# Gate rows of a two-direction mLSTM: one chain over all tokens, or two parts placed by hand

## The chip, the cores and the metric

The kernel runs on one core of one Trainium2 chip. The metric is the time of one execution on the device in microseconds (us), the median over several runs.

## The reference, cut to what matters

One layer of a diffusion backbone acts on 1024 latent tokens (a grid) and 256 context tokens of width 1024. Both are normalised, modulated and projected by one matrix; three branches (pooling, spatial gating, mLSTM) follow, then a merge and a feed-forward part. The change is in the mLSTM branch: four heads, two scan directions, chunked. Its gates, two numbers per token, head and direction, go through the following, in which `b` is a running sum inside a chunk and `m` a running maximum over all chunks:

```python
gp = gate_pre.astype(f32) + b_gates.astype(f32)
i_f, i_b, f_f, f_b = jnp.split(gp, 4, axis=-1)
logf_f = jax.nn.log_sigmoid(f_f)
...
b = jnp.cumsum(fc, axis=1)
dmat = b[:, :, None, :] - b[:, None, :, :] + ic[:, None, :, :]
dmat = jnp.where(causal[None, :, :, None], dmat, -jnp.inf)
inter = b + m[:, None, :]
m_t = jnp.maximum(inter, jnp.max(dmat, axis=2))
w_intra = jnp.exp(dmat - m_t[:, :, None, :])
w_inter = jnp.exp(inter - m_t)
...
w_state = jnp.exp(bL[:, None, :] - b + ic - m_new[:, None, :])
decay = jnp.exp(bL + m - m_new)
```

The head's output is multiplied by `sigmoid(o_pre)`, the output gate. The latent scan starts from a cached state, the context scan from zero.

## The kernel before, in words

Tokens lie in three groups (`GROUPS`): 0 and 1 hold 512 latent (sample) tokens each, 2 holds the 256 context tokens. The normalised input is kept transposed as `uT`, eight blocks of 128 features for each group, each split into a high and a low part, because every product is three matmuls in a narrow float format (`dense`, L117 to 125): high by high, high by low, low by high. A weight block comes by one transfer on SP's queue (`fetch_w`), is rounded to its high part by ScalarE (`A.copy`, L93) and its low part is taken by VectorE (L94). Two raw buffers and three pairs of high and low parts exist (`NRAW`, `NHL`). `dense` writes one of three PSUM banks (`ps_mm`), which ScalarE evicts; transposes and small products use five others (`ps_sd`).

What sets the order: a scheduler reads the program, plays it against a model of the engines and writes each engine's instructions in the order in which they became ready there; among those that are ready the earlier in the program goes first. `Pinned` (L35 to 45) takes that freedom away: an instruction issued through it is queued behind whatever stood before it in the program on its engine. From L258 to L411 the names `V`, `A`, `G`, `PE` are pinned, so that stretch runs in the order in which it is written, and whatever is issued without the wrapper may be put between. All pinned instructions carry the wrapper's line, L43, in the profile.

The pinned stretch computes the modulation, fills `uT` and has k and v of head 0 (`p_k`, `p_v`) multiplied as `uT` comes in. The loop at L376 goes over `steps`: the eight blocks of group 1, then the eight of group 2 (the context steps). A step issues the transposes of the step four ahead (`tr`), the scaling of the step two ahead (`mc`) and six matmuls of k and v. At context step 0 the gates of groups 0 and 1 are multiplied (`gates_of`), copied out by ScalarE (`pgs`) and partly moved to other partitions by a transfer (`pgl`, L357); at context step 3 `gates_add` joins the parts into two rows of `z`. Behind the loop come the evictions of k and v and the gates of group 2.

At L412 the pinning ends. The gate rows' chain (L413 to 470) then runs over all 1280 tokens at once, on 36 partitions (rows 0 to 3 for the forward direction, 32 to 35 for the backward one): Abs, Sigmoid, Exp, Ln on ScalarE, arithmetic and scans on VectorE; the log-sigmoid's correction term is multiplied by the Sigmoid (L421, L426). `zi`, `z5` and `z4` are the three results. Each is transposed in 10 pieces on TensorE (`pc`, L478) and copied into `gcol` by VectorE; a small product (`pd`, L491) spreads two rows of 10 chunks each to all partitions. Then `rhl` splits one more row for later use.

The heads follow (L532 to 662): `head_proj` multiplies what is missing of k, v, q (for head 0 the second and third group of q), and `head` transposes k and v (`tk`, `tv`), sums the states (`kv`), multiplies scores and values (`st`, `rb`, `pv`), and at group 0 of each head issues the output gate's projection (L647, `p_o`), whose eviction `ev_o` writes the Sigmoid into `so`. All of this is the scheduler's to place: where TensorE would wait in its model, it takes matmuls of later program lines.

Of the kernel before, what the change touches and what calls it, by code (L numbers as in the profile page):

```python
# [48 lines left out]
def hybrid_step(  # L49
# [28 lines left out]
    def ps_sd(name):  # L78
        return pp.tile([P, 512], F32, tag="sd", name=name, bufs=5)
# [258 lines left out]
    nc.gpsimd.dma_start(sel, sel8)  # L338

    R36 = 36  # L340
    zr = [z[0:R36, i * T : (i + 1) * T] for i in range(7)]

    gparts = {}

    def gates_of(g):


        t0, n = GROUPS[g]
        pg = ps_sd(f"pg{g}")
# [26 lines left out]
    for at, (g, k) in enumerate(steps):  # L376
# [38 lines left out]
    def chunks(ap):
        return ap.rearrange("p (c t) -> p c t", t=P)

    zi, zf, z2, z3, z4, z5, z6 = zr
    V.tensor_scalar(zf, zf, bgt[:, 1:2], None, ALU.add)
    A.activation(z2, zf, AF.Abs)  # L420
    A.activation(z6, z2, AF.Sigmoid)  # L421
    A.activation(z2, z2, AF.Exp, scale=-1.0)
    V.tensor_scalar(z3, z2, 1.0, None, ALU.add)
    A.activation(z4, z3, AF.Ln)
    V.scalar_tensor_tensor(z5, z3, -1.0, z2, ALU.add, ALU.subtract)
    V.tensor_tensor(z5, z5, z6, ALU.mult)  # L426
    V.tensor_tensor(z4, z4, z5, ALU.subtract)
    V.scalar_tensor_tensor(zf, zf, 0.0, z4, ALU.min, ALU.subtract)
    G.memset(z4, 1.0)
    G.memset(chunks(z4)[0:32, :, 0:1], 0.0)  # L430
    G.memset(chunks(z4)[32:36, :, 127:128], 0.0)
    rev = slice(None, None, -1)
    V.tensor_tensor_scan(z2[0:32], z4[0:32], zf[0:32], 0.0, ALU.mult, ALU.add)
    V.tensor_tensor_scan(z2[32:36, rev], z4[32:36, rev], zf[32:36, rev], 0.0, ALU.mult, ALU.add)
    for lo_, hi_, smp in ((0, NSAMP, True), (NSAMP, T, False)):
        ini = m0t if smp else None
        V.tensor_tensor_scan(
            z3[0:32, lo_:hi_], zf[0:32, lo_:hi_], zi[0:32, lo_:hi_],
            ini[0:32] if smp else 0.0, ALU.add, ALU.max)
        V.tensor_tensor_scan(  # L440
            z3[32:36, lo_:hi_][:, rev], zf[32:36, lo_:hi_][:, rev], zi[32:36, lo_:hi_][:, rev],
            ini[32:36] if smp else 0.0, ALU.add, ALU.max)
    bL = cp.tile([R36, NT], F32, name="bL")
    mnew = cp.tile([R36, NT], F32, name="mnew")
    mprev = cp.tile([R36, NT], F32, name="mprev")
    V.memset(mprev, 0.0)
    b3, m3 = chunks(z2), chunks(z3)
    V.tensor_copy(bL[0:32], b3[0:32, :, 127])
    V.tensor_copy(bL[32:36], b3[32:36, :, 0])
    V.tensor_copy(mnew[0:32], m3[0:32, :, 127])  # L450
    V.tensor_copy(mnew[32:36], m3[32:36, :, 0])
    V.tensor_copy(mprev[0:32, 0:1], m0t[0:32])
    V.tensor_copy(mprev[0:32, 1:8], mnew[0:32, 0:7])
    V.tensor_copy(mprev[0:32, 9:10], mnew[0:32, 8:9])
    V.tensor_copy(mprev[32:36, 7:8], m0t[32:36])
    V.tensor_copy(mprev[32:36, 0:7], mnew[32:36, 1:8])
    V.tensor_copy(mprev[32:36, 8:9], mnew[32:36, 9:10])
    G.dma_start(m_out[0], mnew[0:4, 9:10])
    G.dma_start(m_out[1], mnew[32:36, 8:9])
    bm = cp.tile([R36, NT], F32, name="bm")  # L460
    V.tensor_tensor(bm, bL, mnew, ALU.subtract)
    dec = cp.tile([R36, NT], F32, name="dec")
    V.tensor_tensor(dec, bm, mprev, ALU.add)
    A.activation(dec, dec, AF.Exp)

    V.tensor_tensor(zi, zi, z2, ALU.subtract)
    V.tensor_tensor(z2, z2, z3, ALU.subtract)
    A.activation(z5, z3, AF.Exp, scale=-1.0)
    V.tensor_tensor(chunks(z4), chunks(zi), bm.unsqueeze(2).to_broadcast([R36, NT, P]), ALU.add)
    A.activation(z4, z4, AF.Exp)  # L470


    gcol = cp.tile([P, 3, NT, 8], F32, name="gcol")
    for qi, src in enumerate((zi, z5, z4)):
        pc = ps_sd(f"pc{qi}")
        pcv = pc[:, 0 : NT * R36].rearrange("p (c j) -> p c j", j=R36)
        for c in range(NT):
            PE.transpose(pcv[:, c, :], src[:, c * P : (c + 1) * P], ident[0:R36, 0:R36])  # L478
        for d in range(2):
            V.tensor_copy(gcol[:, qi, :, 4 * d : 4 * d + 4], pcv[:, :, 32 * d : 32 * d + 4])  # L480
    GC, EM, EWS = (gcol[:, i] for i in range(3))

    dsel = tmp("dsel")[0:R36, 0:160].rearrange("p (q j c) -> p q j c", q=2, j=8)
    for qi, src in enumerate((dec, mprev)):
        V.tensor_tensor(
            dsel[:, qi], src.unsqueeze(1).to_broadcast([R36, 8, NT]),
            sel[0:36, :].unsqueeze(2).to_broadcast([R36, 8, NT]), ALU.mult)
    ones36 = tmp("ones36")[0:R36, 0:P]
    V.memset(ones36, 1.0)
    pd = ps_sd("pd")  # L490
    PE.matmul(pd[:, 0:160], ones36, dsel.rearrange("p q j c -> p (q j c)"), start=True, stop=True)  # L491
# [44 lines left out]
    so = z[:, 7730:9010]  # L536
# [18 lines left out]
    def head(h, kT, vT, qT):  # L555
# [980 lines left out]
```

## Time and profile before

| what | us |
|---|---|
| median of three runs | 1947.19 (1946.92 to 1949.57) |
| the profiled execution | 1947.31 |
| its span, first to last instruction | 1945.5 |
| TensorE busy in the span | 1903.0 |
| VectorE busy | 1294.0 |
| ScalarE busy | 861.7 |
| mean granted clock of TensorE | 0.994 of full |

Times inside the trace count from the span's first instruction. In the rows PE is TensorE, DVE VectorE, ACT ScalarE, POOL GpSimd, SP the queue that issues most transfers. A row of a timeline gives the start, the length, the engine, the line of the kernel, the operation with what it writes and reads, and in brackets how long the engine was idle before it and what ended that. Consecutive lengths on TensorE overlap, so the distance of two starts is the price of a matmul. The clock of a window is a share of full speed: TensorE has two levels, 2.4 GHz (1.00) and 1.2 GHz (0.50).

### The profile page before, as it was taken

The numbers are of one execution on the slowest core, as the hardware profiler recorded it, in microseconds if no ns is written. First come the engines' busy times: TensorE is split into PE (matmuls) and PEld (weight loads), VectorE is DVE, ScalarE is ACT, GpSimd is POOL, SyncE is SP. The second block draws the span as 40 slices with busy tenths as digits, with TensorE's granted clock in tenths as the row PEclk, the third lists the DMA queues.
The fourth block names the chain that finished last, engine by engine and source line by source line (L and its number), as shares of the span: only waits on it lengthen the run. The fifth ranks groups of instructions, "written<-read, shape, count | busy, mean of one in ns | idle before, by whom it ended". The sixth has DMA issues, their size and how long they took to land.

```text
span 1945.5 us, 28129 instructions
## 1 busy us (share of the span) xinstructions
PE 1903.0 (98%) x10136; PEld 1627.5 (84%) x10136; DVE 1294.0 (67%) x2207; ACT 861.7 (44%) x1768; POOL 378.2 (19%) x380
## 2 busy tenths in 40 slices
PE   6999999999999999999999999999999999999998
PEld 3778888998788888888888887888888888888886
DVE  6574443347759889875675599888776655744665
ACT  7444464653243333343123374555454545443443
POOL 1200001107302424220000015444431110000003
PEclk9999999999999999999999999999999999999999
DMA  9211111012635445469522435776773586654444
GB/s 361 85 59 33 43 39 40 27 56 70 203 119 165 149 158 164 153 211 321 163 97 98 152 120 212 253 264 246 259 269 136 193 333 203 210 170 151 165 133 159
DMA packets 149318, 313.32 MB, mean 161 GB/s; under 512 B 17550, under 2 KB 40818, under 8 KB 147130
## 3 DMA queue, kind: packets, MB, share of 16 engines
q1 hardware_dynamic: 107354, 220.73, 33.9%
q0 software_dynamic: 15520, 57.75, 7.8%
q10 hardware_dynamic: 26304, 33.04, 4.7%
q8 instruction: 79, 1.29, 0.3%
q14 instruction: 61, 0.50, 0.1%
HBM read 217.59 MB, written 93.36 MB: 160 GB/s over the span
## 4 chain that ended last, share of the span: by engine, by line
PE 87%; DVE 4%; DMA 3%; POOL 2%; ACT 1%; issue 1%; SPq 0%; POOLq 0%; ACTq 0%; DVEq 0%
PE w L1403 6%; PE w L1404 6%; PE w L1405 6%; PE pb L1050 3%; PE pb L1051 3%; PE pb L1052 3%; PE fT L892 3%; PE fT L890 3%; PE fT L891 3%; PE fB L891 2%; PE fB L890 2%; PE fB L892 2%; PE fT_g L892 2%; PE fT_g L890 2%; PE fT_g L891 2%; PE po L1168 2%
## 5 line engine op out<-in xcount | busy, mean ns | idle before, releaser
L1242 POOL TENSOR_TENSOR z<-z 128x512 f32<-128x512 f32 x64 | 100.1, 1564 | 123.3 <-DMA z<-in_w_ff 120.6
L947 DVE TENSOR_TENSOR z<-z 128x512 f32<-128x512 f32 x112 | 88.7, 792 | 2.5
L527 POOL PARTITION_ALL_REDUCE acc<-acc x16 | 54.6, 3446 | 184.0 <-DVE acc L521 113.6
L521 DVE SCALAR_TENSOR_TENSOR acc<-z,scond,acc 128x512 f32<-128x512 f32 x112 | 86.1, 816 | 0.0
L1357 POOL TENSOR_TENSOR rs_y<-rs_y,neghalf 128x1 f32<-128x1 f32 x10 | 9.6, 966 | 333.0 <-DVE rs_y L1356 333.0
L1208 ACT ACTIVATE z<-z 128x512 f32<-128x512 f32 x64 | 40.5, 632 | 69.8 <-DVE z L956 36.7
L972 ACT ACTIVATE z<-z 128x512 f32<-128x512 f32 x48 | 30.3, 632 | 59.1 <-DVE z L956 23.1
L130 POOL TENSOR_TENSOR rs_h<-rs_h,neghalf 128x4 f32<-128x4 f32 (+1 forms) x12 | 10.9, 910 | 200.5 <-DVE rs_h L129 200.3
L653 DVE SCALAR_TENSOR_TENSOR yc<-th,ccol,z 128x512 f32<-128x512 f32 (+1 forms) x12 | 7.9, 661 | 58.2 <-PE th L651 58.2
L1056 DVE TENSOR_TENSOR sg<-pb,sg 128x512 f32<-128x512 f32 (+1 forms) x48 | 28.7, 600 | 26.7 <-PE pb L1052 26.5
L881 ACT CAST hi_wb<-raw_wb 128x512 fp32r<-128x512 f32 x24 | 14.8, 620 | 64.4 <-PE pb L1051 37.6
L1209 ACT ACTIVATE z<-z 128x512 f32<-128x512 f32 x64 | 40.3, 629 | 1.1
L1171 DVE TENSOR_TENSOR po<-po,gt 128x512 f32<-128x512 f32 (+1 forms) x24 | 14.6, 607 | 35.1 <-PE po L1170 35.0
L1233 POOL DMA_DIRECT2D scr_s<-x x48 | 26.3, 549 | 53.1 <-DVE x L1227 47.6
L738 POOL TENSOR_TENSOR z<-z 128x1024 f32<-128x1024 f32 (+13 forms) x20 | 33.6, 1702 | 6.9 <-ACT z L722 4.6
L528 POOL TENSOR_TENSOR acc<-acc,bt 1x512 f32<-1x512 f32 x16 | 23.5, 1480 | 58.4 <-issue 58.4
L1174 ACT ACTIVATE po<-z 128x512 f32<-128x512 f32 (+1 forms) x24 | 12.7, 529 | 48.5 <-DVE z L1173 34.2
L587 DVE SCALAR_TENSOR_TENSOR z<-z,dmb,kv 128x129 f32<-128x129 f32 x56 | 16.6, 345 | 21.8 <-PE kv L576 21.3
L1057 DVE TENSOR_TENSOR z<-z,sg 128x512 f32<-128x512 f32 (+1 forms) x48 | 28.7, 601 | 1.2
L640 DVE TENSOR_TENSOR den<-den,gcol 128x2 f32<-128x2 f32 x40 | 6.2, 159 | 31.0 <-ACT den L639 29.9
L43 PE MATMUL pm<-wah,shl 128*4 128x512 f32 x32 | 13.8, 461 | 13.2 <-ACT wah L43 13.2
L130 POOL TENSOR_TENSOR rs_f<-rs_f,neghalf 128x4 f32<-128x4 f32 (+1 forms) x3 | 3.3, 1092 | 116.9 <-DVE rs_f L129 116.9
(5136 smaller groups left out, 7288.9 us busy)
## 6 DMA issues: line engine op xcount, KB each, us to landing
z<-in_w_ff SPq DMA_DIRECT2D x64, 512.0 KB, 5.5
z<-in_w_ada SPq DMA_DIRECT2D x64, 256.0 KB, 3.1
scr_t<-z POOLq DMA_DIRECT2D x16, 1024.0 KB, 4.9
z<-in_w_in SPq DMA_DIRECT2D x24, 512.0 KB, 4.3
scr_g<-z ACTq DMA_DIRECT2D x48, 256.0 KB, 2.0
sg<-scr_g SPq DMA_DIRECT2D x48, 256.0 KB, 4.5
scr_h<-z ACTq DMA_DIRECT2D x48, 256.0 KB, 3.6
scr_s<-x POOLq DMA_DIRECT2D x48, 256.0 KB, 4.3
```

Of the source, the lines that this page charges most:

```text
L521: V.scalar_tensor_tensor(acc[j], raw, scond[:, k, j : j + 1], acc[j], ALU.mult, ALU.add)
L890: PE.matmul(ps, whi[:, s], ahi, start=first and k == ks[0], stop=False)
L891: PE.matmul(ps, whi[:, s], alo, start=False, stop=False)
L892: PE.matmul(ps, wlo[:, s], ahi, start=False, stop=end and k == ks[-1])
L947: V.tensor_tensor(out, x, y, op)
L1050: PE.matmul(pb[:, :n], whi[:, s], yh, start=kc == 0, stop=False)
L1051: PE.matmul(pb[:, :n], whi[:, s], yl, start=False, stop=False)
L1052: PE.matmul(pb[:, :n], wlo[:, s], yh, start=False, stop=kc == 3)
L1242: G.tensor_tensor(out, x, y, ALU.subtract)
L1403: PE.matmul(banks[j], h_[:, s], rh, start=fp == 0, stop=False)
L1404: PE.matmul(banks[j], l_[:, s], rh, start=False, stop=False)
L1405: PE.matmul(banks[j], h_[:, s], rl, start=False, stop=fp == NFP - 1)
```

## The change

The gate rows' chain becomes ten small functions that take a part: `SMP` (groups 0 and 1, 1024 tokens) or `CTXT` (group 2, 256 tokens). The pinned stretch is lengthened over the whole chain, over the rest of q0, over head 0's output gate (`o0`, taken out of `head(0)`) and over head 1's k (`k1`, taken out of `head_proj(1)` by way of `begun`), so the order between these is the one written. The sample part's first steps stand at context step 6; its transposes stand between `o0` and `k1`, those of the context part behind `k1`. The Sigmoid of the log-sigmoid's correction and its multiplication are left out, and seven rows of `z` become six. The row of ones in the running sum is written by POOL earlier, and the loads and splits of the weights of `o0` and `k1` are traced inside the pinned stretch, but not pinned themselves.

```diff
-    zr = [z[0:R36, i * T : (i + 1) * T] for i in range(7)]
+    zr = [z[0:R36, i * T : (i + 1) * T] for i in range(6)]
...
+    def part(groups):
+        lo_, hi_ = GROUPS[groups[0]][0], sum(GROUPS[groups[-1]])
+        return slice(lo_ // P, hi_ // P), [t[:, lo_:hi_] for t in zr]
+
+    SMP, CTXT = (0, 1), (2,)
...
+    def g_join(groups):
+        for g in groups:
+            gates_add(g)
+        V.tensor_scalar(yf, yf, bgt[:, 1:2], None, ALU.add)
+        engines[2].memset(y4, 1.0)
+        engines[2].memset(chunks(y4)[0:32, :, 0:1], 0.0)
+        engines[2].memset(chunks(y4)[32:36, :, 127:128], 0.0)
+    def g_exp(groups):
+        A.activation(y2, yf, AF.Abs)
+        A.activation(y2, y2, AF.Exp, scale=-1.0)
+    def g_one(groups):
+        V.tensor_scalar(y3, y2, 1.0, None, ALU.add)
+        V.scalar_tensor_tensor(y5, y3, -1.0, y2, ALU.add, ALU.subtract)
+    def g_log(groups):
+        A.activation(y3, y3, AF.Ln)
+    def g_logf(groups):
+        V.tensor_tensor(y3, y3, y5, ALU.subtract)
+        V.scalar_tensor_tensor(yf, yf, 0.0, y3, ALU.min, ALU.subtract)
+    def g_max(groups):
+        for r, d in scan_dirs():
+            V.tensor_tensor_scan(
+                y3[r][:, d], yf[r][:, d], yi[r][:, d], m0t[r] if groups is SMP else 0.0, ALU.add, ALU.max)
+    def g_sum(groups):
+        cc, (yi, yf, y2, y3, y4, y5) = part(groups)
+        c0, c1 = cc.start, cc.stop
+        for r, d in scan_dirs():
+            V.tensor_tensor_scan(y2[r][:, d], y4[r][:, d], yf[r][:, d], 0.0, ALU.mult, ALU.add)
+        b3, m3 = chunks(y2), chunks(y3)
+        V.tensor_copy(bL[0:32, cc], b3[0:32, :, 127])
+        V.tensor_copy(bL[32:36, cc], b3[32:36, :, 0])
+        V.tensor_copy(mnew[0:32, cc], m3[0:32, :, 127])
+        V.tensor_copy(mnew[32:36, cc], m3[32:36, :, 0])
+        if groups is SMP:
+            V.tensor_copy(mprev[0:32, 0:1], m0t[0:32])
+            V.tensor_copy(mprev[32:36, 7:8], m0t[32:36])
...
+        V.tensor_tensor(bm[:, cc], bL[:, cc], mnew[:, cc], ALU.subtract)
+        V.tensor_tensor(dec[:, cc], bm[:, cc], mprev[:, cc], ALU.add)
+    def g_em(groups):
+        A.activation(y5, y3, AF.Exp, scale=-1.0)
+    def g_diff(groups):
+        cc, (yi, yf, y2, y3, y4, y5) = part(groups)
+        V.tensor_tensor(yi, yi, y2, ALU.subtract)
+        V.tensor_tensor(
+            chunks(y4), chunks(yi), bm[:, cc].unsqueeze(2).to_broadcast([R36, cc.stop - cc.start, P]), ALU.add)
+        V.tensor_tensor(y2, y2, y3, ALU.subtract)
+    def g_last(groups):
+        cc, (yi, yf, y2, y3, y4, y5) = part(groups)
+        A.activation(y4, y4, AF.Exp)
+        A.activation(dec[:, cc], dec[:, cc], AF.Exp)
+    def gate_columns(groups):
+        cc, (yi, yf, y2, y3, y4, y5) = part(groups)
+        c0, nch = cc.start, cc.stop - cc.start
+        for qi, src in enumerate((yi, y5, y4)):
+            pc = ps_sd(f"pc{qi}_{c0}")
+            pcv = pc[:, 0 : nch * R36].rearrange("p (c j) -> p c j", j=R36)
+            for c in range(nch):
+                PE.transpose(pcv[:, c, :], src[:, c * P : (c + 1) * P], ident[0:R36, 0:R36])
+            for d in range(2):
+                V.tensor_copy(gcol[:, qi, cc, 4 * d : 4 * d + 4], pcv[:, :, 32 * d : 32 * d + 4])
+        dsel = tmp(f"dsel{c0}")[0:R36, 0 : 16 * nch].rearrange("p (q j c) -> p q j c", q=2, j=8)
+        for qi, src in enumerate((dec, mprev)):
+            V.tensor_tensor(
+                dsel[:, qi], src[:, cc].unsqueeze(1).to_broadcast([R36, 8, nch]),
+                sel[0:36, :].unsqueeze(2).to_broadcast([R36, 8, nch]), ALU.mult)
+        ones36 = tmp(f"ones36_{c0}")[0:R36, 0:P]
+        V.memset(ones36, 1.0)
+        pd = ps_sd(f"pd{c0}")
+        PE.matmul(pd[:, 0 : 16 * nch], ones36, dsel.rearrange("p q j c -> p (q j c)"), start=True, stop=True)
+        V.tensor_copy(
+            dmb[:, :, :, cc], pd[:, 0 : 16 * nch].rearrange("p (q j c) -> p q j c", q=2, j=8))
 
...
-        if (g, k) == (2, 3):
-            gates_add(0)
-            gates_add(1)
+        if (g, k) == (2, 6):
+            g_join(SMP)
+            g_exp(SMP)
+            g_one(SMP)
+            g_log(SMP)
+            g_logf(SMP)
...
+    def ev_o(g, ps):
+        t0, n = GROUPS[g]
+        A.activation(so[:, t0 : t0 + n], ps[:, :n], AF.Sigmoid)
+    def q0_part(g):
+        ps = ps_mm(f"p_q0{g}")
+        dense(ps, w_q0, uT, g)
+        begun["q0"][1].append(evict_kqv("q", 0, g, ps, kq0))
+    def o0_part(g):
+        ps = ps_mm(f"p_o0{g}")
+        dense(ps, w_o0, uT, g)
+        ev_o(g, ps)
+    pinned, (V, A, G, PE) = (V, A, G, PE), engines
+    kq1 = slot("kq1", F32)
+    w_o0 = load_w(w_in[I_O], "o0")
+    w_k1 = load_w(w_in[I_K + 1], "k1")
+    begun["k1"] = w_k1, []
+    V, A, G, PE = pinned
+    g_join(CTXT)
+    g_exp(CTXT)
+    g_max(SMP)
+    g_one(CTXT)
+    g_sum(SMP)
+    q0_part(1)
+    q0_part(2)
+    g_log(CTXT)
+    g_em(SMP)
+    g_diff(SMP)
+    o0_part(0)
+    g_last(SMP)
+    o0_part(1)
+    o0_part(2)
+    gate_columns(SMP)
+    g_logf(CTXT)
+    g_max(CTXT)
+    g_sum(CTXT)
+    g_em(CTXT)
+    g_diff(CTXT)
+    g_last(CTXT)
+    for g in range(3):
+        ps = ps_mm(f"p_k1{g}")
+        dense(ps, w_k1, uT, g)
+        begun["k1"][1].append(evict_kqv("k", 1, g, ps, kq1))
+    gate_columns(CTXT)
     V, A, G, PE = engines
-    gates_add(2)
...
-    A.activation(z6, z2, AF.Sigmoid)
...
-    V.tensor_tensor(z5, z5, z6, ALU.mult)
...
-            if g == 0:
+            if g == 0 and h > 0:
                 proj(I_O + h, f"o{h}", ev_o)
```

## Rows read from the trace of the kernel before

**Rows 1.** Page, part 1: busy time, share of the span and instructions of each engine.
```profile
PE 1903.0 (98%) x10136; PEld 1627.5 (84%) x10136; DVE 1294.0 (67%) x2207; ACT 861.7 (44%) x1768; POOL 378.2 (19%) x380
```

**Rows 2.** Waits of TensorE, 60 to 160 us: us in total, times, longest.
```profile
PE pc L478 <- DVE z L466: 3.6, 1, 3.6
...
PE p_v L43 <- ACT kT L43: 1.1, 1, 1.1
...
PE p_k L123 <- ACT z L597: 0.3, 1, 0.3
```

**Rows 3.** Windows: busy us by engine, granted clock, DMA share, GB/s.
```profile
80.00:90.00 10.00, 8.94 (x53) 7.71 (x52) 2.62 (x7) 4.64 (x10) 0.00 (x0) 1.00 0.15 43
...
130.00:135.00 5.00, 1.38 (x16) 1.20 (x15) 4.80 (x12) 0.00 (x0) 1.07 (x2) 0.98 0.01 0
...
135.00:140.00 5.00, 5.00 (x26) 4.64 (x26) 4.97 (x15) 2.39 (x4) 0.00 (x0) 0.50 0.08 16
...
140.00:145.00 5.00, 5.00 (x26) 3.86 (x26) 2.14 (x3) 0.31 (x2) 0.00 (x0) 0.84 0.32 87
```

**Rows 4.** Timeline of TensorE, 85 to 147 us: start, length, line, operation, idle before.
```profile
88.65 0.48 PE L43 MATMUL p_k<-u2c,hi_k 128*128 128x256 f32 x2
...
89.58 0.47 PE L123 MATMUL p_q<-u0h,hi_q 128*128 128x512 f32 x1
...
98.75 0.40 PE L43 MATMUL pg<-u0c,wgs 128*128 128x256 f32 x2
...
100.67 0.28 PE L123 MATMUL p_q<-u0c,hi_q 128*128 128x256 f32 x1
...
103.56 0.40 PE L123 MATMUL p_o<-u0h,hi_o 128*128 128x512 f32 x1
...
109.02 0.39 PE L123 MATMUL p_o<-u0h,hi_o 128*128 128x512 f32 x1
...
134.29 1.97 PE L478 MATMUL pc<-cst,z 36*128 36x36 f32 x20 [3.62 <-DVE z L466]
...
144.37 0.81 PE L478 MATMUL pc<-cst,z 36*128 36x36 f32 x10
```

**Rows 5.** Timeline of VectorE, 85 to 147 us.
```profile
89.37 0.73 DVE L43 SCALAR_TENSOR_TENSOR z<-pgs,bgt,pgl 36x512 f32<-36x512 f32 x1
...
104.89 0.48 DVE L363 SCALAR_TENSOR_TENSOR z<-pgs,bgt,pgl 36x256 f32<-36x256 f32 x1 [1.26 <-DMA pgl<-pgs]
...
105.83 0.88 DVE L419 TENSOR_SCALAR z<-z,bgt 36x1280 f32<-36x1280 f32 x1
...
118.94 2.34 DVE L437 TENSOR_TENSOR_SCAN z<-z,m0t 32x1024 f32<-32x1024 f32 x1
...
126.21 2.81 DVE L433 TENSOR_TENSOR_SCAN z<-z 32x1280 f32<-32x1280 f32 x1
...
131.89 0.16 DVE L450 COPY mnew<-z 32x10 f32<-32x10 f32 x1
...
132.66 1.48 DVE L466 TENSOR_TENSOR z<-z 36x1280 f32<-36x1280 f32 x1
```

**Rows 6.** Timeline of ScalarE, 85 to 147 us.
```profile
89.91 0.57 ACT L43 ACTIVATE val_u<-pt_u,sh,a 128x256 f32<-128x256 f32 x1 [0.37 <-PE pt_u L43]
...
100.91 0.38 ACT L43 COPY pgs<-pg 128x256 f32<-128x256 f32 x1
...
109.34 1.28 ACT L422 ACT_TABLE_LOAD   x1
...
110.64 1.27 ACT L422 ACTIVATE z<-z 36x1280 f32<-36x1280 f32 x1
```

**Rows 7.** Windows of 2 us around another wait of TensorE.
```profile
1158.00:1160.00 2.00, 0.88 (x4) 0.89 (x5) 1.14 (x4) 1.60 (x5) 0.26 (x1) 0.69 0.36 137
...
1160.00:1162.00 2.00, 1.98 (x10) 1.60 (x8) 1.26 (x4) 2.00 (x6) 0.00 (x0) 0.50 0.65 223
```

**Rows 8.** Timeline of TensorE at that wait.
```profile
1159.12 2.39 PE L1142 MATMUL pt<-cst,xn 128*128 128x128 f32 x10 [3.03 <-ACT xn L1134]
```

More of the change, by code (lines that the diff above doesn't have):

```diff
@@ L364, in gates_add, with chunks @@
         V.tensor_tensor(zr[1][:, t0 : t0 + n], both[64:100], low[64:100], ALU.add)
+    def chunks(ap):
+        return ap.rearrange("p (c t) -> p c t", t=P)
+    zi, zf, z2, z3, z4, z5 = zr
+    rev = slice(None, None, -1)
+    bL = cp.tile([R36, NT], F32, name="bL")
+    mnew = cp.tile([R36, NT], F32, name="mnew")
+    mprev = cp.tile([R36, NT], F32, name="mprev")
+    bm = cp.tile([R36, NT], F32, name="bm")
+    dec = cp.tile([R36, NT], F32, name="dec")
+    gcol = cp.tile([P, 3, NT, 8], F32, name="gcol")
@@ new lines, in hybrid_step, with scan_dirs @@
+    GC, EM, EWS = (gcol[:, i] for i in range(3))
+    dmb = cp.tile([P, 2, 8, NT], F32, name="dmb")
+    decb, mpb = dmb[:, 0], dmb[:, 1]
+    V.memset(mprev, 0.0)
+    def part(groups):
+        lo_, hi_ = GROUPS[groups[0]][0], sum(GROUPS[groups[-1]])
+        return slice(lo_ // P, hi_ // P), [t[:, lo_:hi_] for t in zr]
+    SMP, CTXT = (0, 1), (2,)
+    def scan_dirs():
+        return (slice(0, 32), slice(None)), (slice(32, 36), rev)
+    def g_join(groups):
+        _, (yi, yf, y2, y3, y4, y5) = part(groups)
+        for g in groups:
[4 more added lines that the diff above has]
+        engines[2].memset(chunks(y4)[32:36, :, 127:128], 0.0)
@@ new lines, in g_exp @@
+    def g_exp(groups):
+        _, (yi, yf, y2, y3, y4, y5) = part(groups)
+        A.activation(y2, yf, AF.Abs)
+        A.activation(y2, y2, AF.Exp, scale=-1.0)
+    def g_one(groups):
+        _, (yi, yf, y2, y3, y4, y5) = part(groups)
+        V.tensor_scalar(y3, y2, 1.0, None, ALU.add)
+        V.scalar_tensor_tensor(y5, y3, -1.0, y2, ALU.add, ALU.subtract)
+    def g_log(groups):
+        _, (yi, yf, y2, y3, y4, y5) = part(groups)
+        A.activation(y3, y3, AF.Ln)
+    def g_logf(groups):
+        _, (yi, yf, y2, y3, y4, y5) = part(groups)
+        V.tensor_tensor(y3, y3, y5, ALU.subtract)
+        V.scalar_tensor_tensor(yf, yf, 0.0, y3, ALU.min, ALU.subtract)
@@ new lines, in g_max @@
+    def g_max(groups):
+        _, (yi, yf, y2, y3, y4, y5) = part(groups)
+        for r, d in scan_dirs():
[14 more added lines that the diff above has]
+            V.tensor_copy(mprev[32:36, 7:8], m0t[32:36])
+        V.tensor_copy(mprev[0:32, c0 + 1 : c1], mnew[0:32, c0 : c1 - 1])
+        V.tensor_copy(mprev[32:36, c0 : c1 - 1], mnew[32:36, c0 + 1 : c1])
+        if groups is CTXT:
+            engines[2].dma_start(m_out[0], mnew[0:4, 9:10])
+            engines[2].dma_start(m_out[1], mnew[32:36, 8:9])
+        V.tensor_tensor(bm[:, cc], bL[:, cc], mnew[:, cc], ALU.subtract)
+        V.tensor_tensor(dec[:, cc], bm[:, cc], mprev[:, cc], ALU.add)
@@ new lines, in g_em @@
+    def g_em(groups):
+        _, (yi, yf, y2, y3, y4, y5) = part(groups)
+        A.activation(y5, y3, AF.Exp, scale=-1.0)
[9 more added lines that the diff above has]
+        A.activation(dec[:, cc], dec[:, cc], AF.Exp)
@@ L411, in hybrid_step @@
     gates_of(2)
-    V, A, G, PE = engines
-    gates_add(2)
[L415 to L420, printed above, removed]
-    A.activation(z6, z2, AF.Sigmoid)
[L422 to L425, printed above, removed]
@@ L426, in hybrid_step @@
-    V.tensor_tensor(z5, z5, z6, ALU.mult)
[L427 to L491, printed above, removed]
@@ L492, in hybrid_step @@
-    dmb = cp.tile([P, 2, 8, NT], F32, name="dmb")
-    V.tensor_copy(dmb.rearrange("p q j c -> p (q j c)"), pd[:, 0:160])
-    decb, mpb = dmb[:, 0], dmb[:, 1]
+    so = z[:, 7730:9010]
+    def ev_o(g, ps):
[9 more added lines that the diff above has]
+        ev_o(g, ps)
@@ L535, in hybrid_step @@
     S = z[:, 5150:7730].rearrange("p (c d t) -> p c d t", d=2, t=129)
-    so = z[:, 7730:9010]
     hn2 = [z[:, 9010 + i * 512 : 9522 + i * 512].rearrange("p (c t) -> p c t", t=P) for i in range(2)]
@@ L593, in head @@
         A.dma_start(st_out[h], fin)
-        def ev_o(g, ps):
-            t0, n = GROUPS[g]
-            A.activation(so[:, t0 : t0 + n], ps[:, :n], AF.Sigmoid)
         ssq = small([P, 16], f"ssq{h}")
```

## The prediction

> **What bounds the kernel now.** I read the engines' busy times first: TensorE is busy 98% of the span and VectorE 67% [rows 1]. So the order of TensorE's work decides, and an edit to the gate rows, which VectorE and ScalarE compute, counts only where TensorE waits for them or slows because of them. TensorE's own waits between 60 and 160 us come next: three entries, one of them large. The transposes of the gate rows (pc, L478) wait 3.6 us for VectorE's zi (L466); the others are 1.1 us (p_v for an eviction) and 0.3 us (p_k for the sigmoid of o0) [rows 2]. The windows then show a second price. From 135 to 140 us the granted clock is 0.50, from 140 to 145 us 0.84 [rows 3]: the idle stretch from 130.7 us was followed by the lower of the two levels, 1.2 GHz. That costs 0.5 x 5 + 0.16 x 5 = 3.3 us of full-speed time. So the stage loses 3.6 + 3.3 + 0.3 = 7.2 us that better placing could give back, 0.37% of the time. The 1.1 us at 86 us lies ahead of everything that the change touches and stays.
>
> **What the change moves, and what it does not.** It is said to put the output gate and head 1's k in front of the transposes. In the timeline they were there: p_o's first group starts at 103.56 us and its second at 109.02 us [rows 4], while pc comes at 134.29 us and p_k shares the half-speed stretch. The scheduler had done this unasked. TensorE's amount of work stays too (30 transposes of 36 rows as 24 and 6, the one small matmul becomes two). What is left is the question when the sample tokens' rows are ready, against when TensorE, now in a fixed order, gets to them. I work out both clocks.
>
> **TensorE's clock after the change.** Context step 2 of the pinned loop starts at 88.65 us; today a part of q0's second group stands between the steps (from 89.58 us) [rows 4], and pinned it comes behind the gates. A 256-column matmul takes 0.12 us (q0's last group: 24 from 100.67 to 103.56 us). Six steps of six matmuls, with two transposes left among them, end at about 93.05 us. Gates of group 2: 98.75 to 100.67 is 1.9 us, so 95.0. Second q0 group: 5.5 us, as p_o's first (103.56 to 109.02), so 100.5. Last q0 group 2.9, o0 5.5 + 5.5 + 2.9: 117.2 us without waits.
>
> **VectorE and ScalarE, sample part.** The last context column's scaling ends at 90.5 us [rows 6], its split on VectorE at 91.2. The join no longer stands in front of the splits: four adds of some 0.73 us [rows 5] end at 94.15. Rows over 1280 columns are scaled by 0.8 for 1024 columns and by 0.2 for 256; that is an estimate, but the 512- and 1280-column rows (0.73 and 1.48 us) lie on that line. Bias add 0.88 x 0.8 = 0.7: 94.85. Abs 1.0, table load 1.28, Exp 1.0 [rows 6]: 98.2. Load for Ln 1.28 and Ln 1.0: 100.5, with VectorE's two steps beside it. Only then, in ScalarE's fixed order, come the evictions of k0 and v0 and the copy of group 2's gates, spaced 0.3 us: k0's bank is free at 100.8, so q0's last group waits **0.5 us** with the bank's release; the copy ends at 101.45. Its two edits of order cancel: group 2's gates leave TensorE 5.7 us earlier, but their copy ends when it does today (100.91 + 0.38) [rows 6]. From there to the add that waits for SP's transfer it was 3.6 us (104.89) [rows 5], so join, 1.2 us, ends at 106.1 and ScalarE's context Abs and Exp at 108.1. Behind these two wait q0's two evictions; the first ends at 108.7. The second o0 group needs that bank at 109.6: 0.9 us to spare, so nothing.
> VectorE goes on: two max scans of 2.34, the context's two short steps 0.7, two adding scans of 2.81 x 0.8, ten small copies and sums spaced 0.19, and zi, 1.48 x 0.8 [rows 5]: 106.1 + 4.7 + 0.7 + 4.5 + 1.9 + 1.2 = **119.1 us**. TensorE is there at 117.2 + 0.5 = 117.7 and waits **1.4 us**. The eight transposes of zi and the eight of the second row take 0.6 each (10 in 0.81) [rows 4] and end at 120.3. The third row is zi plus bm, 1.2, then Exp, 1.0: 121.3, a wait of **1.0 us**. Behind its transposes (121.9) stand VectorE's copies out of PSUM, two products with sel and a memset, some 0.9 us, and TensorE's next matmul, pd, needs them. Unpinned work, head 0's transposes among it, can stand in there; between 0 and 0.9 I take **0.45 us**. Then k1 runs for 14 us and covers the context rows' rest (about 7 us on VectorE). All of it is less a removed wait than a wait cut into pieces.
>
> **What costs nothing.** The Sigmoid and the multiplication that go (a pass over all 1280 columns each) are off this sum already. POOL's memsets and the two m_out transfers are on an idle engine. The casts and splits of o0's and k1's weights fit in while VectorE waits for Exp and for the transfer; without that cover each delays zi by a pass over 1024 columns, some 1.2 us. SP's queue carries the same loads, and the gates' transfer keeps its time. Five table loads more (nine instead of four) lie beside TensorE as long as the eviction of q0 keeps its 0.9 us.
>
> **The clock afterwards.** From 117.7 to 122.9 us TensorE would do little: 2.9 us idle and small transposes. The nearest rows are a wait of 3.0 us behind which ten transposes and matmuls ran: 0.69 and 0.50 in two windows of 2 us, (0.31 + 0.50) x 2 = **1.6 us** [rows 7, 8]. The ends are 0, as around the 1.1 us wait (1.00 from 80 to 90 us), and 3.3 us, as today [rows 3]. My pieces together come nearest to the 3.0 us wait, so 1.6.
>
> **Sum.** 0.5 + 1.4 + 1.0 + 0.45 + 1.6 = 4.95 us paid for 7.2 us given back: 2.25 us gained. The profiled execution took 1947.31 us (its span is 1945.5 us), 0.12 us above the median, so 1945.1 us. With the clock's two ends it is 1943.5 and 1946.8 us; with a weight split of some 1.2 us in the chain besides, 1948.
>
> **Rivals.**
> (1) *The stall goes altogether.* The scheduler sets v1's matmuls, which are not pinned, or head 0's transposes into the gaps, or zi is 1.5 us earlier than I count. Paid is 0.5 alone: 1940.6 us. For it: today it slots pc into the middle of p_k, so it does interleave. Against it: it misjudged pc by 3.6 us, and v1 needs its low half from a VectorE that has no gap.
> (2) *ScalarE becomes the bound: slower.* Its waits are now in a fixed order with evictions behind each. It decides once q0's first eviction ends after 109.6 us, 0.9 us later than counted. If a switch of tables cost twice its row, 2.56 us, k0's eviction would come at 103.4 (TensorE waits 2.9), q0's at 112.4 (0.7), zi at 121.7 (0.9), the third row's Exp, behind two more switches, at 126.0 (3.1), pd 0.9: 8.5 us, and with 3.3 us of half clock 11.8 paid for 7.2: 1951.9 us. Casts that fall in the chain would do the same. Against it: the rows show the Exp 0.02 us behind its load (109.34 + 1.28 to 110.64) [rows 6].
> The Trainium skill (ScalarE: Activation LUTs, "What ACT_TABLE_LOAD costs") gives a switch 1.28 us of load and 1.38 us of drain and advises to batch by table set, which speaks against this change; by it this rival would hold. The trace agrees with the load and shows no drain behind it.
> (3) *It comes to the same.* The transposes wait as long as before, in other pieces, and the clock falls for as long: 1947.3 us. The two projections were in front already, which speaks for it.
>
> **How the numbers follow.** Forecast 0.40, rival (1) 0.31, (2) 0.17, (3) 0.12. A measurement of this kernel can tell about 0.2%, 3.9 us, from no change: below 1943.3 and above 1951.1 us. Faster: all of (1) and 0.07 of the forecast, where the clock holds: 0.38. Slower: most of (2), 0.16. Same: 0.46. Everything behind 145 us is scheduled anew from these times, which may shift each case by one or two microseconds. The range, 1939.8 to 1951.2 us, takes in (1) with such a shift and leaves out the larger part of (2). The forecast's own range is 1942.5 to 1948.
>
> **What would show it.** Right: TensorE waits for zi and for the third row between 115 and 125 us, 1 to 2 us each, the granted clock falls for some 3 us behind them, and no wait is left at the context's transposes. Rival (1): 1.00 in all windows there and no pc wait over 0.5 us. Rival (2): waits of p_q or p_o for ScalarE's evictions. Wrong in the first step: if group 2's gates are copied well before 101 us, the whole chain moves ahead.

## The result and the profile after

The changed kernel takes 1954.95 us (median of 16 runs, 1950.67 to 1959.04) where the kernel before, run beside it, takes 1948.19 us (16 runs): a ratio of 1.0031, with an interval of 1.0024 to 1.0038. It is 0.3% slower, 6.8 us, where 2.25 us of gain was forecast, and it lies above the whole range.

The profiled execution took 1954.39 us, its span is 1952.6 us. Part 1 of its page stands against [rows 1]:

```profile
PE 1903.4 (97%) x10138; PEld 1626.9 (83%) x10138; DVE 1298.6 (67%) x2232; ACT 867.6 (44%) x1778; POOL 381.8 (20%) x383
```

TensorE has the same work, 0.4 us more of 1903. The span is 7.1 us longer, so nearly all of the difference, 6.7 us, is time in which TensorE stands. Where it arises, two instructions tell that both kernels have: the first matmul of the gates and the last transposes at the end of the four heads. TensorE's timeline of the kernel before:

```profile
78.06 0.39 PE L43 MATMUL pg<-u0h,wgs 128*128 128x512 f32 x1
...
452.27 0.38 PE L651 MATMUL th<-cst,z 128*128 128x128 f32 x2
```

and of the changed kernel:

```profile
77.64 0.39 PE L43 MATMUL pg<-u0h,wgs 128*128 128x512 f32 x1
...
458.83 0.38 PE L737 MATMUL th<-cst,z 128*128 128x128 f32 x2
```

From the one to the other it was 374.2 us and is 381.2 us: the whole 7.0 us lie in this stage (called "the stage" below, measured so for each kernel). The heads behind it are alike: from 165 to 460 us TensorE has the same three waits in both kernels (1.2, 0.9 and 0.7 us), and the granted clock is 1.00 throughout. TensorE's waits of the changed kernel from 60 to 165 us, against [rows 2]:

```profile
PE pd L43 <- DVE ones L43: 3.8, 1, 3.8
PE pc L43 <- ACT z L43: 2.3, 1, 2.3
PE p_q L43 <- ACT kq L43: 2.3, 1, 2.3
PE pc L43 <- DVE z L43: 1.5, 1, 1.5
```

The one wait of 3.6 us has become four, 9.9 us together (with the 0.3 us of p_k it was 3.9 before, apart from the p_v wait of 1.1 us at 86 us in both, and from 0.2 us at 71 us here, ahead of the stage). The changed kernel's windows, against [rows 3]:

```profile
120.00:125.00 5.00, 1.66 (x20) 1.55 (x21) 3.62 (x7) 2.77 (x4) 0.00 (x0) 0.69 0.07 15
125.00:130.00 5.00, 1.18 (x9) 1.03 (x7) 1.82 (x6) 4.05 (x5) 0.00 (x0) 0.50 0.11 20
130.00:135.00 5.00, 5.00 (x13) 3.80 (x12) 4.44 (x12) 0.42 (x1) 0.00 (x0) 0.50 0.27 98
135.00:140.00 5.00, 5.00 (x22) 4.11 (x21) 2.59 (x9) 1.11 (x3) 1.07 (x2) 0.95 0.01 0
```

TensorE is busy for 2.8 of the 10 us from 120 to 130, and its clock stands at the lower level from about 122 to 135.5 us, where before it was from about 135 to 141.5 us. TensorE's timeline, against [rows 4]:

```profile
92.83 0.40 PE L43 MATMUL pg<-u0c,wgs 128*128 128x256 f32 x2
...
102.62 0.51 PE L43 MATMUL p_q<-u0c,hi_q 128*128 128x256 f32 x2 [2.25 <-ACT kq L43]
...
121.02 1.27 PE L43 MATMUL pc<-cst,z 36*128 36x36 f32 x16 [1.47 <-DVE z L43]
124.61 1.06 PE L43 MATMUL pc<-cst,z 36*128 36x36 f32 x8 [2.32 <-ACT z L43]
129.49 0.76 PE L43 MATMUL pd<-dsel,ones 36*128 36x128 f32 x2 [3.82 <-DVE ones L43]
130.19 0.79 PE L43 MATMUL p_k<-u0h,hi_k 128*128 128x512 f32 x1
...
135.47 0.43 PE L43 MATMUL p_k<-u4h,hi_k 128*128 128x512 f32 x1
```

The gates of group 2 start at 92.83 us, where 93.05 was forecast; from there on each of the four waits can be read off what VectorE and ScalarE did. VectorE's timeline, against [rows 5]:

```profile
93.90 1.22 DVE L94 TENSOR_TENSOR lo_o<-raw_o,hi_o 128x1024 fp32r<-128x1024 f32 x1
95.04 0.74 DVE L43 TENSOR_SCALAR z<-z,bgt 36x1024 f32<-36x1024 f32 x1
...
100.00 1.22 DVE L43 SCALAR_TENSOR_TENSOR z<-z 36x1024 f32<-36x1024 f32 x1
...
106.87 4.69 DVE L43 TENSOR_TENSOR_SCAN z<-z,m0t 32x1024 f32<-32x1024 f32 x2
111.59 1.23 DVE L94 TENSOR_TENSOR lo_v<-raw_v,hi_v 128x1024 fp32r<-128x1024 f32 x1
...
123.19 0.47 DVE L43 COPY gcol<-pc 128x32 f32<-128x32 f32 x4
127.52 1.23 DVE L94 TENSOR_TENSOR lo_q<-raw_q,hi_q 128x1024 fp32r<-128x1024 f32 x1 [3.87 <-ACT hi_q L93]
128.67 0.28 DVE L43 COPY gcol<-pc 128x32 f32<-128x32 f32 x2
```

and ScalarE's, against [rows 6]:

```profile
101.25 1.06 ACT L43 ACTIVATE z<-z 36x1024 f32<-36x1024 f32 x1 [0.70 <-DVE z L43]
102.21 0.36 ACT L43 ACTIVATE kq<-p_k 128x256 f32<-128x256 f32 x1
...
122.20 1.28 ACT L43 ACT_TABLE_LOAD   x1 [4.02 <-DVE z L43]
123.50 1.06 ACT L43 ACTIVATE z<-z 36x1024 f32<-36x1024 f32 x1
...
124.67 1.28 ACT L43 ACT_TABLE_LOAD   x1
125.96 0.60 ACT L43 ACTIVATE z<-p_o 128x512 f32<-128x512 f32 x1
126.45 1.04 ACT L93 CAST hi_q<-raw_q 128x1024 fp32r<-128x1024 f32 x1
```

- **q0's last group, 2.25 us.** It needs the bank that ScalarE empties at 102.21, behind Ln (101.25). Ln writes its result over the row that VectorE's correction step (100.00 to 101.22) still reads, so it waited 0.70 us for that step; and the whole chain was 1.1 us late because the scheduler had set the split lo_o, which is not pinned, in front of the bias add (95.04 instead of 93.90).
- **zi, 1.47 us.** The split lo_v (111.59, 1.23 us) lies in the chain, behind the max scans. What it costs is read from its length; the one attempt to take it out (experiment 2) put another delay in its place.
- **The third row, 2.32 us.** The table load for its Exp stood idle until the row was there (122.20) instead of going ahead; 1.28 us of load lie in the chain.
- **The small product, 3.82 us.** The split lo_q of head 1's q stands between VectorE's copies of the first two results and those of the third. It waited 3.87 us for its cast (126.45), which on ScalarE stood behind two Exps, a table load and the eviction of o0. Everything behind it on VectorE, and pd on TensorE, waited with it.

### The profile page after: what moved, and what is told of

Same layout as the page of the kernel before. It is cut to its first block, busy times and chain, and to the rows that moved or that the text cites. A ratio compares the mean times of both kernels' runs of the same rounds, so it can differ in the third digit from the quotient of the medians.

```text
span 1952.6 us, 28176 instructions
## 1 busy us (share of the span) xinstructions
PE 1903.4 (97%) x10138; PEld 1626.9 (83%) x10138; DVE 1298.6 (67%) x2232; ACT 867.6 (44%) x1778; POOL 381.8 (20%) x383
## 4 chain that ended last, share of the span: by engine, by line
PE 84%; DVE 6%; DMA 3%; issue 2%; ACT 2%; POOL 1%; SPq 0%; ACTq 0%; POOLq 0%; DVEq 0%
PE w L1489 6%; PE w L1490 6%; PE w L1491 6%; PE fT L978 3%; PE fT L976 3%; PE fT L977 3%; PE pb L1137 3%; PE pb L1136 3%; PE pb L1138 3%; PE fB L978 2%; PE fB L976 2%; PE fB L977 2%; PE po L1254 2%; PE po L1255 2%; PE po L1256 2%
## 5 line engine op out<-in xcount | busy, mean ns | idle before, releaser
L1033 DVE TENSOR_TENSOR z<-z 128x512 f32<-128x512 f32 x112 | 95.1, 849 | 2.5
```

Source lines behind the costliest of these rows:

```text
L1033: V.tensor_tensor(out, x, y, op)
```

## The experiments

All ratios are to the kernel before, run on the same chip in the same session; 9 to 12 runs of each kernel, 22 or 33 of the kernel before. The stage is read from one profiled execution of each kernel, the ratio from all its runs. Runs of one kernel spread by several us (the kernel before from 1945.81 to 1956.71 us in one session), and in experiments 4 and 5 the stage is 2.2 and 3.5 us above before while the ratio is level: a few us of the stage count only with a named wait or the ratio beside them. The theories carry letters in the expectations; A is mine: unpinned weight splits and the in-order placing of the chain cost the time, not the amount of work.

**1. lo_q taken off VectorE.** The split of head 1's q goes to GpSimd, all else as in the change.

```diff
-            proj(idx + h, ..., w=w, groups=range(len(lst), 3))
+            proj(idx + h, ..., w=w, groups=range(len(lst), 3),
+                 eng=G if f"{nm}{h}" in ("q1",) else V)
```

> Edit: the low part of head 1's q weights is taken by GpSimd instead of VectorE; nothing else. Theory A (the changed kernel's largest wait is this split, lo_q, which the scheduler set on VectorE between the copies of zi's and of the third row's transposes, where it waits for ScalarE's cast): the wait of pd falls from 3.8 us to about 0.9 us, the order of all else stays, and the time falls by about 3 us, to some 0.15 to 0.2% above before. Rival B (pd waits for the third row's Exp and what stands behind it on ScalarE anyway): pd waits 3 us or more as now, and the time stays at 0.3% above before.

Measured: 1951.49 us, ratio 1.0011 (1.0002 to 1.002). The wait for pd falls from 3.82 to 0.87 us; TensorE's timeline of this kernel:

```profile
127.63 0.77 PE L43 MATMUL pd<-dsel,ones 36*128 36x128 f32 x2 [0.87 <-DVE ones L43]
```

The stage falls from 381.2 to 378.3 us, by the same 2.9 us. So A held, and the one split costs 2.9 of the 7 us. VectorE's order was otherwise unchanged.

**2. lo_v on GpSimd too** (`("v1", "q1")` in the line above).

> Edit: the low parts of head 1's v and q weights are both taken by GpSimd. Theory A: besides what the split of q gives back, lo_v (1.23 us) leaves the chain between the max scans and the context's short steps, so zi and all behind it come 1.2 us earlier and the first pc wait falls from 1.5 to about 0.3 us; the time is about 4 us below the changed kernel, 0.1% above before. Rival B: as for the split of q alone, and zi earlier by 1.2 us, but the wait at pd longer by as much: no gain over the changed kernel.

Measured: 1951.61 us, 1.001 (1.0001 to 1.0019), no better than the first, which A did not expect; the stage is 378.9 us. The wait for zi grew, to 2.55 us, though VectorE had one step less. This kernel's VectorE timeline:

```profile
106.88 6.87 DVE L43 TENSOR_TENSOR_SCAN z<-z,m0t 32x1024 f32<-32x1024 f32 x2
...
129.05 2.48 DVE L43 SCALAR_TENSOR_TENSOR z<-z 36x256 f32<-36x256 f32 x1
```

and its GpSimd timeline:

```profile
106.86 2.39 POOL L94 TENSOR_TENSOR lo_v<-raw_v,hi_v 128x1024 fp32r<-128x1024 f32 x1 [33.72 <-ACT hi_v L93]
128.63 2.62 POOL L94 TENSOR_TENSOR lo_q<-raw_q,hi_q 128x1024 fp32r<-128x1024 f32 x1 [19.38 <-ACT hi_q L93]
```

Both times GpSimd works, the VectorE step beside it is longer by about its length: the two scans 6.87 us against 4.69 in the change, the step at 129.05 2.48 us against 0.42. The split was not out of the chain; it held it from the other engine. The Trainium skill (SBUF — State Buffer, "Who interferes with whom") says that a VectorE instruction with two inputs in SBUF contends with a GpSimd instruction that reads SBUF, and calls the port pair that the two share an exclusive lock. These four rows agree.

**3. The evictions of k0 and v0 in front of Ln**, to take away the 2.25 us.

```diff
-            g_log(SMP)
-            g_logf(SMP)
...
     gates_of(2)
+    g_log(SMP)
+    g_logf(SMP)
```

> Edit: in ScalarE's written order the evictions of k0 and v0 and the copy of group 2's gates come before the sample part's Ln instead of behind it. Theory A (the chain decides, the wait only moves): the 2.25 us wait of q0's last group goes, the gates of group 2 are copied 3 us earlier, but VectorE is busy with the sample part until 105 us, so zi comes only some 0.9 us earlier and the first pc wait grows from 1.5 to about 2.9 us; the time falls by about 1 us. Rival C (the banks' evictions are what costs): the 2.25 us are won, 0.2% above before.

Measured: 1954.23 us, 1.0021 (1.0012 to 1.0029). The wait of p_q is gone, but zi's is 3.2 us now, and those of the third row and of pd stay at 2.4 and 3.8 us; waits 9.4 us together, stage 379.2 us, 2.0 below the change. Its timeline of TensorE and one of its windows:

```profile
128.33 0.77 PE L43 MATMUL pd<-dsel,ones 36*128 36x128 f32 x2 [3.83 <-DVE ones L43]
```

```profile
130.00:135.00 5.00, 5.00 (x20) 4.00 (x19) 4.67 (x15) 0.42 (x1) 1.07 (x2) 0.82 0.11 43
```

Counted from the gates' first matmul (77.26 us here), pd starts at 51.1 us where it was 51.9 in the change: of the 2.25 us only 0.8 get through, the rest hid later waits, as A has it. The other 1.2 us of the stage came with the clock, which rose earlier (0.82 in this window, 0.50 in the change). In time it is thus C's figure that came out, 0.2% above before, and not A's; in the waits it is A's.

**4. A group of head 1's k in front of the transposes**, to give the chain more cover.

```diff
     o0_part(2)
+    k1_part(0)
     gate_columns(SMP)
...
+    k1_part(1)
+    k1_part(2)
```

> Edit: the first of the three groups of head 1's k stands in front of the sample part's transposes instead of behind them. Theory A (the rows are late by less than the 5.5 us that this group takes): both pc waits, 1.5 and 2.3 us, go, the clock does not fall, and what is left is a pd wait of up to 3 us from lo_q; the time is 6 to 8 us below the changed kernel, within 0.1% of before. Rival D (the heads that follow need the sample columns early, so the work put ahead is paid back there): the waits go from the pc transposes, but others of the same length appear between 130 and 200 us, and the time stays at 0.3% above before.

Measured: 1949.0 us, 0.9997 (0.9988 to 1.0005): 6 us below the change, level with before. As A has it, and against D, both waits of the transposes are gone; p_q keeps 2.3 us and pd 1.9 us. The stage is 376.5 us, still 2.2 us above before, for the clock fell twice, which A did not expect: to 0.89 and 0.77 from 100 to 110 us behind the wait of p_q, and to 0.62 and 0.70 from 130 to 140 us.

**5. The two parts, not pinned.** The chain stays cut in two; from the join of the context part on, its order is left to the scheduler.

```diff
-    V, A, G, PE = pinned
     g_join(CTXT)
```

> Edit: the two parts and their small steps stay, but from the context's join on the instructions are left to the scheduler instead of being kept in the written order (the sample part's first steps stay pinned). Theory A (the fixed order is what hurts, because TensorE can no longer be given other work while a row is late): the scheduler sets other work in the gaps, TensorE's waits from 100 to 130 us fall from 9.9 us to that of before or below, some 4 us, and the time is within 0.2% of before. Rival E (the chain in two parts is itself longer, by its nine table loads and twice the small steps, whoever orders it): the waits stay above 8 us and the time 0.3% above before.

Measured: 1949.31 us, 0.9997 (0.9988 to 1.0006); p_q waits 3.0 us, pc 3.9 us, stage 377.7 us. Without these pins the change costs nothing that can be measured, and it gains nothing either. A's time came out, but its waits did not: 6.9 us remain, where A had some 4 and E over 8.

**6. The kernel before without the Sigmoid.** Two lines leave the kernel before, nothing else.

```diff
-    A.activation(z6, z2, AF.Sigmoid)
...
-    V.tensor_tensor(z5, z5, z6, ALU.mult)
```

> Edit to the kernel before: only the Sigmoid of the log-sigmoid's correction and its multiplication are left out, which is the part of the change that shortens the chain without ordering anything (the correction term is then not weighted). Theory A: the chain is shorter by 1.5 us on VectorE, but the scheduler knows it and places the transposes as much earlier, so TensorE's pc wait stays between 2 and 4 us and the time within 0.1% of before. Rival G: the wait falls by the whole 1.5 us or more and the clock holds, 0.2% or more below before.

Measured: 1951.82 us, 1.0008 (0.9998 to 1.0017); the stage is 374.4 us, as before. Its timeline of TensorE:

```profile
76.74 0.39 PE L43 MATMUL pg<-u0h,wgs 128*128 128x512 f32 x1
...
132.16 2.32 PE L476 MATMUL pc<-cst,z 36*128 36x36 f32 x20 [4.97 <-DVE z L464]
```

Counted from the gates' first matmul, pc starts at 55.4 us instead of 56.2 (134.29 less 78.06), so the results come 0.8 us earlier; but the scheduler puts less in front of them, and pc waits 5.0 us instead of 3.6. Shortening the chain by itself bought nothing, and it cost nothing that shows, which speaks against G; the wait is longer than the 2 to 4 us that A gave.

**7. The Sigmoid of o0's first eviction behind the last Exp**, so that no table load stands before that Exp.

```diff
-    o0_part(0)
     g_last(SMP)
+    o0_part(0)
```

> Edit to the changed kernel: the first eviction of o0 (Sigmoid) is written behind the third row's Exp instead of in front of it, so ScalarE keeps its table between the two sample Exps, two table loads fewer. In the changed kernel the load for that Exp did not go ahead: it waited for VectorE's row like the Exp itself, so 1.28 us of it lay on the path. Theory A: the wait of the third row's transposes falls from 2.3 to about 1.0 us, but pd still waits for the split lo_q, whose cast on ScalarE stands behind two Sigmoids, and that wait grows from 3.8 to about 4.4 us; the time falls by 0.5 to 1 us only. Rival H (the table loads are what makes the change slow): the time falls by 2.5 us or more.

Measured: 1952.82 us, 1.002 (1.0011 to 1.0029). This kernel's ScalarE timeline, the Exp of the third row and what follows:

```profile
121.75 1.06 ACT L43 ACTIVATE z<-z 36x1024 f32<-36x1024 f32 x1 [5.94 <-DVE z L43]
122.72 0.19 ACT L43 ACTIVATE dec<-dec 36x8 f32<-36x8 f32 x1
122.93 1.28 ACT L43 ACT_TABLE_LOAD   x1
```

The Exp follows the row (which VectorE finishes at 121.66) without a load, and the wait of its transposes is 1.16 us instead of 2.32: the load was that wait's other half. But the time goes into pd's wait, 4.70 us instead of 3.82, and the stage, 380.3 us, is only 0.9 us shorter. A held in the waits and the stage; table loads (H) are not the main cause. pd starts 51.1 us behind the gates' first matmul (128.24 less 77.17), as in experiment 3. The wait for zi is gone here for a poor reason: behind the same 2.25 us wait of p_q the clock fell, and q0's last group and o0 took longer.

**8. Four steps together.** Edits 3 and 4, and the loads of head 1's v and q pinned where they hinder nothing: v's cast and split behind the sample part's transposes, q's behind the last of the context part's steps.

```diff
     gate_columns(SMP)
+    begun["v1"] = load_w(w_in[I_V + 1], "v1", eng=V), []
     g_logf(CTXT)
...
     g_last(CTXT)
+    begun["q1"] = load_w(w_in[I_Q + 1], "q1", eng=V), []
```

> Edit to the changed kernel: the first group of head 1's k in front of the sample part's transposes, the evictions before the sample part's Ln, and the casts and splits of head 1's v and q weights written into the fixed order behind the sample part's columns and behind the context's last Exp, on VectorE. Theory A (three causes, each by its length: the bank's wait, unpinned splits in the chain, rows needed 2 to 4 us too early): no p_q wait, no pc wait, a pd wait of 0.9 us; between the gates' first matmul and the last head's last transpose it is 9 to 12 us shorter than the changed kernel and 2 to 5 us shorter than before; the time is 0.1 to 0.25% below before. Rival D (what is put ahead is paid back in the heads): waits appear between 130 and 200 us and the time is within 0.1% of before.

Measured: 1945.06 us (1944.5 to 1946.14), ratio 0.9975 (0.9965 to 0.9985): the best of all, 0.25% below the kernel before and 0.56 points of ratio below the change. TensorE's only wait from 90 to 150 us in this kernel:

```profile
PE pd L43 <- DVE ones L43: 0.9, 1, 0.9
```

Its timeline of TensorE:

```profile
123.05 1.67 PE L43 MATMUL pc<-cst,z 36*128 36x36 f32 x24
125.60 0.46 PE L43 MATMUL pd<-dsel,ones 36*128 36x128 f32 x2 [0.87 <-DVE ones L43]
...
448.34 0.38 PE L743 MATMUL th<-cst,z 128*128 128x128 f32 x2
```

and its windows:

```profile
120.00:125.00 5.00, 4.72 (x38) 3.81 (x36) 2.91 (x9) 3.92 (x5) 0.00 (x0) 1.00 0.00 2
125.00:130.00 5.00, 4.40 (x13) 3.46 (x14) 3.53 (x10) 3.38 (x5) 0.00 (x0) 0.66 0.28 40
130.00:135.00 5.00, 5.00 (x31) 4.44 (x30) 4.21 (x14) 1.23 (x4) 1.07 (x2) 1.00 0.24 95
```

All 24 transposes run as one, without a wait, and the stage (from 78.29 us) is 370.1 us, 4.2 below before and 11.1 below the change. A held in all its figures, and D's waits from 130 to 200 us are not there. The clock still falls, for one window. How much each of the steps adds was not run, apart from edits 3 and 4 by themselves.

**9. pd behind a further group of k1**, so that its last wait is covered as well (from 8; the small product becomes `gate_factors`).

```diff
     gate_columns(SMP)
+    k1_part(1)
+    gate_factors(SMP)
```

> Edit: as the run before it, and besides the small product of the chunk factors (pd) is taken out from behind the columns' transposes and put behind the second group of head 1's k. Theory A: the last 0.9 us wait goes too and the granted clock stays at 1.00 between 110 and 150 us; another 1 to 3 us below the run before it, 0.2 to 0.35% below before. Rival F (the transposes alone, 24 in a row, let the clock fall whatever stands behind them): the wait goes, but the clock falls as before, and only 1 us is won.

Measured: 1947.93 us, 0.9994 (0.9983 to 1.0004), worse than 8. pd waits no more; 0.73 us fall on k1's next group, which waits for an eviction of o0. The clock falls all the same, to 0.89 and 0.76 from 120 to 130 us, behind the 24 transposes and that wait. A missed. F foresaw the fall, but not that nothing would be won, and with a wait beside the transposes again its reason is not shown. The stage is 373.1 us.

**10. pd in front of the transposes** (from 8; the sel products, the memset and pd moved to the head of `gate_columns`).

> Edit to the run with k1's first group ahead and the weights pinned: the two products with sel, the memset and pd stand in front of the columns' transposes instead of behind them, since the factors are ready when TensorE gets there. Theory A: the 0.9 us wait of pd goes and no new wait comes, 0.5 to 1.5 us below that run, 0.3% below before. Rival F (a stretch of 24 small transposes lets the clock fall even without a wait): the wait goes and the clock still falls to 0.5 for about 3 us behind them, so no more than 0.9 us is won.

Measured: 1947.18 us, 0.999 (0.9979 to 1.0001). pd waits 1.0 us in its new place: its products with sel wait for the chunk factors (dec), whose Exp stands behind the third row's on ScalarE. VectorE's timeline:

```profile
122.08 0.22 DVE L43 TENSOR_TENSOR dsel<-dec,sel 36x64 f32<-36x64 f32 x1 [1.42 <-ACT dec L43]
```

So the factors were not ready when TensorE got there, as A had assumed. The clock is 0.91, 0.50 and 0.91 in the three windows from 120 us, and the stage is 372.1 us. A missed here too: no gain over 8. F had no wait and some 3 us of lower clock; the wait is there, and the clock is down for some 6 us. Why 9 and 10 lose 2 to 3 us in the stage against 8 is not settled: the clock is part of it, and everything behind is scheduled anew.

## Why the prediction was wrong

The sum's own steps, in us, beside what the profile of the changed kernel has:

| term of "Sum" | forecast | measured |
|---|---|---|
| q0's last group for k0's bank | 0.5 | 2.25 |
| transposes for zi | 1.4 | 1.47 |
| transposes for the third row | 1.0 | 2.32 |
| pd for VectorE | 0.45 | 3.82 |
| lower clock | 1.6 | some 3.4 |
| paid | 4.95 | 13.3 |

The clock's figure is worked out: from 130.19 to 135.47 us k1's matmuls start every 0.43 us instead of 0.23, which is half of 5.28 us; the last eight transposes (1.06 us, a third of 1.67 in experiment 8) and pd (0.76 against 0.46) add 0.5 and 0.3. With 7.2 us given back as forecast this makes 6.1 us slower; the stage shows 7.0. The 0.9 us left are not assigned.

- **"What costs nothing": the step that failed.** "The casts and splits of o0's and k1's weights fit in while VectorE waits": o0's did not, the scheduler set lo_o in front of the bias add. And the list was short: once k1 has moved up, v1's and q1's splits come due in the same stretch. I had priced a split as its own length, 1.2 us; lo_q cost 2.9 us (experiment 1), because it waits for its cast and holds all of VectorE's pinned steps behind it. The term that it hit, pd, was bounded by 0 and 0.9 us, for which I had looked at the work between the transposes and pd, not at what else may stand in VectorE's queue there.
- **"With VectorE's two steps beside it."** They are not beside Ln: one reads the row that Ln overwrites. That (0.70 us) and lo_o (1.1 us) move the end of k0's eviction from 100.8 us to 102.57 (102.21 + 0.36), and the wait becomes 2.25 us. Experiment 3 shows that taking it away alone brings pd forward by 0.8 us only.
- **The third row.** I took its table load to go ahead, as the rows show for others (99.27 and 109.89 here: the load runs, then the activation waits). The kernel before had one that did not go ahead, in front of the first eviction of p_o, and it was overlooked. ScalarE's timeline there:

```profile
115.88 1.28 ACT L597 ACT_TABLE_LOAD   x1 [1.38 <-DVE z L426]
```

  By the code, the activations whose load ran ahead depend on VectorE alone; this eviction depends on TensorE's product and on VectorE, which still reads the row beneath, and the Exp of the third row on VectorE's row and on GpSimd's ones beneath it. Whether that is what decides, no run tried; that the load was in the chain experiment 7 shows (1.16 against 2.32 us). The 1.28 us is the length of [rows 6], and no drain shows behind it: 122.20 + 1.28 to 123.50. By the Trainium skill's page (ScalarE: Activation LUTs, "What ACT_TABLE_LOAD costs") 1.38 us more would stand there; the trace does not have them.
- **The clock.** The direction was right, the size was not: 1.6 us was read from one wait of 3.0 us, and here 7.6 us of waits lie between 119.5 and 129.5 us, with the clock down until 135.5 us.
- **What held.** That the two projections were in front already and nothing is gained by naming them; the reading that the wait is cut into pieces; zi's time, 120.87 us against 119.1 with TensorE late by nearly as much; no wait at the context's transposes. Of the rivals, the second comes nearest, by its last sentence, "casts that fall in the chain would do the same": not the doubled table switch that it was worked out with, and not at the evictions that it named, apart from the first. Its price, 1951.9 us, was itself 3 us short.
- **Two figures beneath the sum.** The rows of 512 and 1280 columns (0.73 and 1.48 us) are not proportional to their columns, so scaling by columns is too low for the short ones: steps of 256 columns took 0.41 us, not 0.30, those of 1024 columns 1.21, near the 1.18 of the scaling. And the time at which the second o0 group needs its bank adds up to 109.4 us by the terms given, not 109.6. Neither moved a wait.

## What to carry to other kernels

Pinning some instructions on an in-order engine does not order those that are left free: list every unpinned cast and split that may come due in the stretch, with the producer that it waits for, and pin those too; one that waits holds all that stands behind it. A wait that is removed alone mostly moves to the next one, since TensorE then arrives there earlier: taking away a wait of 2.25 us (experiment 3) and a load of 1.28 us from the chain (experiment 7) brought pd forward by only 0.8 us each. The cutting of the chain gained nothing by itself (0.9997, experiment 5), nor did cover ahead of its end alone (0.9997, experiment 4); with the earlier evictions and the pinned weights as well it was a gain (0.9975). Whether the same cover would serve the chain uncut was not tried. Look in the code for steps that overwrite what another engine still reads before setting two engines side by side.

## What the runs showed of the hardware that was not expected

- A GpSimd operation of 2.39 us with two inputs lengthened two VectorE scans beside it by 2.18 us (6.87 against 4.69), one of 2.62 us a small VectorE step by 2.06 us (2.48 against 0.42), both in experiment 2.
- The same wait of 2.25 us at 102 us had 1.00 behind it in the changed kernel and 0.83 in experiment 7, whose windows are

```profile
100.00:105.00 5.00, 2.85 (x17) 2.85 (x18) 3.18 (x3) 1.92 (x5) 0.00 (x0) 0.83 0.07 22
105.00:110.00 5.00, 5.00 (x24) 4.42 (x23) 4.74 (x5) 3.38 (x5) 0.00 (x0) 0.83 0.00 0
```

  So from a wait's length alone it can't be told here whether the clock falls behind it.
- In experiment 8 a wait of only 0.87 us was followed by a window at 0.66, with 24 transposes of 36 columns just ahead of it. In experiment 10 the wait of 1.0 us stands ahead of the transposes, and the clock fell while they still ran (they run from 123.01 to 124.93 us; 1.00 from 123 to 124 us, 0.54 from 124 to 125), so no wait behind them is needed. Whether the transposes alone would do it is open: in experiments 8, 9 and 10 a wait of 0.7 to 1.0 us stands beside them.
